# Two planes of queries stored at once, the sample item in one pass, a third output tile, and weight loads on another queue

## The chip, the cores and the metric

One core of a Trainium2 chip. The metric is the device time of one execution in microseconds (us); lower is better. The kernel before has a median of 3264.86 us in three runs (3264.8 to 3269.89).

## What is computed

A two-layer encoder step on 2048 prompt frames and 64 new frames ("sample") that follow 2048 past frames held in caches. Model width 1024, 16 heads of 64, all in float32. Layer A attends within bands of chunks (softmax with a bias by distance); layer B is a stick-breaking attention over shared keys and values.

```python
def band_attend(q, k, v, q_pos, k_pos, rel_bias):      # layer A
    s = jnp.einsum('bqhd,bkhd->bhqk', q, k).astype(jnp.float32) * SCALE
...
    s = s + rel_bias[:, rel].astype(jnp.float32)[None]
...
    p = jax.nn.softmax(s, axis=-1).astype(v.dtype)
    return jnp.einsum('bhqk,bkhd->bqhd', p, v)

def sb_block(q, k, v, q_pos, k_pos):                   # layer B
    z = jnp.einsum('bqhd,bkhd->bhqk', q, k).astype(jnp.float32) * SCALE
    mask = (k_pos[None, :] < q_pos[:, None])[None, None]
    log_fail = jnp.where(mask, jax.nn.log_sigmoid(-z), 0.0)
    later = jnp.flip(jnp.cumsum(jnp.flip(log_fail, -1), axis=-1), -1) - log_fail
    w = jnp.where(mask, jnp.exp(jax.nn.log_sigmoid(z) + later), 0.0)
    return jnp.einsum('bhqk,bkhd->bqhd', w.astype(v.dtype), v)
```

Each layer: an RMS norm, projections to q, k, v and a gate, attention, output times SiLU(gate), an output projection and the residual. The outputs are y for prompt and sample and the new key and value rows of both layers.

## The kernel before

Every float32 operand of a matmul is split in a rounded part (hi) and its rest (lo), so a product is two or three matmuls. Heads are taken in eight pairs (HP). The stages follow one another: A's projections (0 to 690 us of the span), A's attention (690 to 1310), B's projections (1310 to 2015), B's attention (2015 to 3156) and the last output tiles. Projections write q, k, v and gates to scratch in DRAM; attention loads them back.

**Scratch and stores.** q has three planes in DRAM: hi, lo, and hi once more (`lay`, `put` at L234), so that the two halves of a query tile can each be loaded as two neighbouring planes (`load_q`, L523: partitions 0 to 63 get hi and lo, 64 to 127 get lo and hi). `put` issues one DMA for a plane: three for q, two for k. The projections keep a half of the frames for one pair in tiles `sh` and `sl` (pool `st`, five buffers, L367); the cache's keys are turned on PE (`ps_c`) and split into `kh` and `kl` (`stage_cache`, L431).

**Attention.** Each attention runs in two passes, first the frame groups (1, 0) of 512, then (3, 2), over all head pairs. An `item` is a head, a group and (in B) a chunk of keys: scores `z` on PE, then softmax or a scan, turns of the weights (`wt`) on PE, splits `ph`/`pl` by ACT and DVE, products `acc` on PE. `gate_steps` (L603) closes a head: its `shift` moves half of `acc` into `otmp` and, in A, the other half into the output tile `ot` (two buffers), which after the gate is stored (`o_a<-ot`). The 64 new frames are the sample item, one for each head pair. In A it stands in the second pass, with its own bias rows `bs` (L1206) and queries `qs`. In B, `SAMPLE` (L40) divides it: in the first pass it meets the new frames' keys and the newest 512 of the cache (chunks 4 and 3), keeps the carry of its scan and a sum, and in the second pass it meets the other three chunks.

**Work beside it.** Projections that only the second pass needs are "late jobs" (`late_job`, L737): `load` fetches weights `lwh` and `lwl`, `some` multiplies into `ps_j`, `out` makes a gate `sg` or a split tile `sp` and stores it, and in A `add_back` and `token_rows` make the rows `lkn` of an output. In B the late weights were cut in the projections and lie in DRAM; they are loaded from ACT's queue. A class `Beat` deals steps out between items at a set rate.

**What sets the order.** A scheduler orders the instructions of each engine from program order and an estimate of times; within the attentions some are kept in program order. Loads and most stores go out from SP through `Queue` (load L135, store L128); L237 is `put`'s own DMA, and a helper records all the other operations as L91. Each DMA is counted on one of eight counters in turn, so an issue waits until the DMA eight before it on the same queues has landed; an instruction that must wait stops all that stand behind it on its engine. The names DMAHW0 to DMAHW7 below are these counters.

Of the kernel before, what the change touches and what calls it, by code (L numbers as in the profile page):

```python
# [16 lines left out]
P = 128  # L17
# [19 lines left out]

SEEN = 3

SAMPLE = {(1, 0): [4, 3], (3, 2): [2, 1, 0]}  # L40

DEFER = dict(a=[("k", hp) for hp in range(HP)], b=[(k, hp) for k in "gq" for hp in range(HP)])
KEPT = "b"
# [5 lines left out]
HOLD = dict(a=1, b=2)  # L49

STEP = 2
BEHIND = 2

SETTLE = 5
# [47 lines left out]
def encoder_step(ctx: ExitStack, tc: tile.TileContext, a: dict, o: dict):  # L102
# [70 lines left out]
    for L, rows in (("a", CACHE_A), ("b", PAST)):  # L173
        lay[L] = dict(


            q=[dram.tile([3, P, T], F32R, name=f"q_{L}{i}") for i in range(HP)],
            k=[dram.tile([2, P, T + rows], F32R, name=f"k_{L}{i}") for i in range(HP)],

            v=dram.tile([T + rows, H, P], F32R, name=f"v_{L}"),  # L180
            g=[dram.tile([P, T], F32, name=f"gate_{L}{i}") for i in range(HP)],

            o=[dram.tile([HP, P, CH if g < GROUPS else NS], F32, name=f"o_{L}{g}") for g in range(GROUPS + 1)],

            w={x: dram.tile([2, P, NK, P], F32R, name=f"w_{L}{x[0]}{x[1]}") for x in DEFER[L] if L in KEPT},
        )
# [44 lines left out]
            mm(out, sh(k), ml(k), start=False, stop=False)  # L231
            mm(out, sl(k), mh(k), start=False, stop=(k == NK - 1))

    def put(L, kind, hp, s, cols, part, by=nc.sync.dma_start):  # L234

        for i in (0, 2) if kind == "q" and s == 0 else (s,):
            by(f32(lay[L][kind][hp][i, :, cols]), f32(part))  # L237


    def projections(L, x_of, begin, w_v, cv, gv, out_v, jobs, first, prompt, sample, stages):  # L240
        with (
# [122 lines left out]
                                nc.scalar.dma_start(vraw[1 + r0 : 1 + r0 + n, cols], vn[:n])  # L364


            with tc.tile_pool(name=f"st_{L}", bufs=5) as spool, tc.tile_pool(name=f"t_{L}", bufs=2) as pool:  # L367
                for j, (kind, w, c0, g) in enumerate(jobs):
                    for hp in range(HP):
                        for _ in range(-(-len(stages) // (len(jobs) * HP - j * HP - hp))):  # L370
                            stages.pop(0)(pool)

                        home, tag = (pool, "wr") if hp % 2 else (opool, "og")
                        raw = home.tile([P, NK, P], F32, name="wraw", tag=tag, bufs=1)
                        c = c0 + hp * P
                        wh = opool.tile([P, NK, P], F32R, name="wh", tag="oh", bufs=2)
                        wl = opool.tile([P, NK, P], F32R, name="wl", tag="ol", bufs=2)

                        with tc.issue_after(first_copy.ins) if j == 0 and hp < 2 else nullcontext():
                            nc.scalar.dma_start(raw, w[:, c : c + P].rearrange("(k p) c -> p k c", p=P))  # L380
                            scaled_split(wh, wl, raw, g)
                        if (kind, hp) in lay[L]["w"]:
                            for i, part in enumerate((wh, wl)):
                                nc.sync.dma_start(f32(lay[L]["w"][kind, hp][i]), f32(part))
                        for hf, (r0, n, chunks) in enumerate(HALVES):
                            xh, xl = xs[hf]
                            if hf and (kind, hp) in DEFER[L]:

                                continue
                            if kind == "g":  # L390
                                sg = spool.tile([P, 1088], F32, name="sg", tag="st")
                            else:
                                sh = spool.tile([P, 1088], F32R, name="sh", tag="st")
                                sl = spool.tile([P, 1088], F32R, name="sl", tag="st")
                            for c, m in chunks:
                                ps = psum.tile([P, CH], F32, name="ps_t", tag="mm", bufs=5)
                                mm3(
                                    ps[:, :m],
                                    lambda k: wh[:, k],
                                    lambda k: wl[:, k],  # L400
                                    lambda k: xh[:, k, c : c + m],
                                    lambda k: xl[:, k, c : c + m],
                                )
                                if kind == "g":
                                    act.activation(sg[:, c : c + m], ps[:, :m], AF.Silu)
                                else:
                                    split(sh[:, c : c + m], sl[:, c : c + m], ps[:, :m])
                            if kind == "g":
                                nc.sync.dma_start(lay[L]["g"][hp][:, r0 : r0 + n], sg[:, :n])
                                continue  # L410
                            for s, part in enumerate((sh, sl)):
                                put(L, kind, hp, s, slice(r0, r0 + n), part[:, :n])
                            if kind == "k":

                                cols = slice(hp * P, hp * P + P)
                                for c in range(0, HALF, CH):
                                    b = hf * HALF + c - first
                                    if b >= 0:
                                        kf = pool.tile([P, CH], F32, name="kf", tag="kf", bufs=2)
                                        part = slice(c, c + CH)  # L420
                                        gps.tensor_tensor(kf, f32(sh[:, part]), f32(sl[:, part]), ALU.add)
                                        natural(pool, kf, 0, P, 4, prompt[b : b + CH, cols])
                                if hf == 0:
                                    kf = pool.tile([P, CH], F32, name="kf", tag="kf", bufs=2)
                                    part = slice(NEW, NEW + NS)
                                    gps.tensor_tensor(kf[:, :NS], f32(sh[:, part]), f32(sl[:, part]), ALU.add)
                                    natural(pool, kf, 0, NS, 1, sample[:, cols])
# [3 lines left out]
    def stage_cache(L, hp, c, pool):  # L431
# [4 lines left out]
        ps = bank("ps_c")  # L436
        for j in range(4):
            flip(ps[:, j * P : j * P + P], kr[:, j])
        kh = pool.tile([P, CH], F32R, name="kh", tag="kh", bufs=1)
        kl = pool.tile([P, CH], F32R, name="kl", tag="kl", bufs=1)  # L440
        split(kh, kl, ps)
        for s, part in enumerate((kh, kl)):
            put(L, "k", hp, s, to, part)
        if L == "b":
            return
        vr = pool.tile([P, 4, 2, DH], F32, name="vr", tag="vr", bufs=2)
# [76 lines left out]
    def load_q(L, pool, hp, h, q0):  # L523

        there(L, "q", hp, q0)
        q = pool.tile([P, 2, CH], F32R, name="q", tag="q", bufs=3)
        src = f32(lay[L]["q"][hp][:, h * DH : h * DH + DH, place(q0) : place(q0) + CH]).rearrange("s d t -> d s t")
        for s in range(2):
            queue.load(f32(q[s * DH : s * DH + DH]), src[:, s : s + 2])
        return q  # L530

    def load_gate(L, pool, hp, q0):
# [27 lines left out]
    class Sample:  # L560
# [9 lines left out]
        def queries(self, hp):  # L570
            q = self.q[hp % 3]
            for h in range(2):
                rows = slice(h * DH, h * DH + DH)
                src = f32(lay[self.L]["q"][hp][0:2, rows, NEW : NEW + NS])
                queue.load(f32(q[rows, :, rows]), src.rearrange("s d t -> d s t"))
            return q

# [25 lines left out]
    def gate_steps(L, pool, acc, h, c0, n, gt, sums, hp, g):  # L603
# [3 lines left out]

        def shift():
            if "ot" not in sums:
                sums["ot"] = pool.tile([P, CH], F32, name="ot", tag="ot", bufs=2)  # L610
            sums[h] = pool.tile([P, CH], F32, name="otmp", tag="otmp", bufs=1)
            act.activation(sums[h][mine, :n], acc()[other, c0 : c0 + n], AF.Copy)
            if L == "a" and n > NS:
                act.activation(sums["ot"][mine, :n], acc()[mine, c0 : c0 + n], AF.Copy)
# [122 lines left out]
    def late_job(L, kind, w, c0, g, hp, x2, first, prompt, rows_pool):  # L737
        st = {}

        def load():  # L740
# [5 lines left out]
            st["wl"] = opool.tile([P, NK, P], F32R, name="lwl", tag="ol", bufs=2)  # L746
            if L in KEPT:
                for i, part in enumerate((st["wh"], st["wl"])):
                    act.dma_start(f32(part), f32(lay[L]["w"][kind, hp][i]))

        def cut(k0):
            ks = slice(k0, k0 + STEP)
# [12 lines left out]
        def out(c):  # L765
# [7 lines left out]
            else:  # L773
                sp = opool.tile([P, 2, CH], F32R, name="sp", tag="xr", bufs=2)
                split(sp[:, 0], sp[:, 1], ps)
                for s in range(2):
                    put(L, kind, hp, s, at, sp[:, s], queue.store)
                st[c] = sp
            if c + CH == HALF:
                done_late.add((L, kind, hp))  # L780

        def add_back(c):

            st["kn"] = rows_pool.tile([P, CH], F32, name="lkn", tag="lkn", bufs=1)
            gps.tensor_tensor(st["kn"], f32(st[c][:, 0]), f32(st[c][:, 1]), ALU.add)

        def token_rows(c):
# [306 lines left out]
    with (  # L1094
# [106 lines left out]
        def sample_item(hp):  # L1201
            st, sums = {}, {}

            def one():

                bs = pool.tile([P, 576], F32, name="bs", tag="bs", bufs=1)  # L1206
                for h in range(2):
                    queue.load(bs[h * DH : h * DH + DH], biasd[hp][0:DH, h, 0:576])
                q = new.queries(hp)
# [61 lines left out]
    with (  # L1271
# [127 lines left out]
        def items():  # L1399
            for part in ORDER:  # L1400
                for hp in range(HP):
                    kv = {}
                    for g in part:
# [8 lines left out]
                                yield item(hp, g, h, q, gt, sums, kv[c], acc, carry, c)  # L1412
                        if hp == HP - 1:
                            beat.when_summed(partial(summed, g))
                    yield sample_item(hp, SAMPLE[part])
            beat.when_summed(partial(summed, GROUPS))

        def summed(g):
# [137 lines left out]
```

## Time and profile before

| | |
|---|---|
| Median of three runs | 3264.86 us |
| Profiled execution | 3263.8 us, span 3262.0 us |
| Granted TensorE clock, mean | 0.996 |
| DMA traffic | 688.41 MB |
| HBM read, written | 408.78 MB, 276.07 MB |

The span runs from the first to the last instruction that the profiler saw. PE is TensorE's matmuls and PEld its weight loads, DVE is VectorE, ACT ScalarE, POOL GpSimd, and SP the engine that issues most DMAs; SPq and ACTq are queue rows, where a duration is that of issuing and not of the transfer. A row of the timeline has its start, its duration, engine and line, operation, what it writes and reads, and in brackets the idle time of the engine ahead of it and what ended that. A landing time runs from a DMA's issue to its last byte.

### The profile page before, as it was taken

The numbers are of one execution on the slowest core, as the hardware profiler recorded it, in microseconds if no ns is written. First come the engines' busy times: TensorE is split into PE (matmuls) and PEld (weight loads), VectorE is DVE, ScalarE is ACT, GpSimd is POOL, SyncE is SP. The second block draws the span as 40 slices with busy tenths as digits, with TensorE's granted clock in tenths as the row PEclk, the third lists the DMA queues.
The fourth block names the chain that finished last, engine by engine and source line by source line (L and its number), as shares of the span: only waits on it lengthen the run. The fifth ranks groups of instructions, "written<-read, shape, count | busy, mean of one in ns | idle before, by whom it ended". The sixth has DMA issues, their size and how long they took to land.

```text
span 3262.0 us, 53645 instructions
## 1 busy us (share of the span) xinstructions
PE 3197.6 (98%) x17928; PEld 2783.9 (85%) x17928; DVE 1885.5 (58%) x3786; ACT 1709.4 (52%) x3719; POOL 1289.7 (40%) x1950
## 2 busy tenths in 40 slices
PE   8999999999998999999999999999999999999999
PEld 7889999988887898878899998888888888888877
DVE  4235431157778776232044332888878888888873
ACT  5234222258878776143143442666656666666662
POOL 3001110035655554020044200344467777777761
PEclk9999999999999999999999999999999999999999
DMA  6359993388899983453299999987735566355423
GB/s 204 121 185 368 351 333 122 118 251 219 235 266 258 254 231 121 167 185 130 106 349 352 350 353 336 254 219 215 214 117 164 167 203 193 116 144 143 137 72 120
DMA packets 464891, 688.41 MB, mean 211 GB/s; under 512 B 51445, under 2 KB 261397, under 8 KB 464614
## 3 DMA queue, kind: packets, MB, share of 16 engines
q1 hardware_dynamic: 398246, 608.68, 60.0%
q10 hardware_dynamic: 66368, 76.29, 7.3%
q8 instruction: 143, 2.34, 0.3%
q14 instruction: 134, 1.10, 0.1%
HBM read 408.78 MB, written 276.07 MB: 210 GB/s over the span
## 4 chain that ended last, share of the span: by engine, by line
PE 79%; issue 7%; DVE 7%; DMA 3%; ACT 2%; POOL 1%; SPq 0%; ACTq 0%; POOLq 0%; DVEq 0%
PE ps_t L91 24%; PE ps_v L91 11%; PE acc L91 11%; PE z L91 10%; PE wt L91 9%; PE ps_j L91 7%; PE ps_o L91 5%; DVE s L91 3%; DVE pl L91 2%; PE ps_tr L91 1%; DMA woraw<-in_w_out_a 1%; ACT ph L91 1%; PE ps_c L91 1%; POOL s L91 0%; PE ps_n L91 0%
## 5 line engine op out<-in xcount | busy, mean ns | idle before, releaser
L91 DVE TENSOR_TENSOR pl<-wt,ph 128x512 fp32r<-128x512 f32 (+1 forms) x864 | 550.6, 653 | 107.4 <-ACT ph L91 104.2
L91 ACT ACTIVATE ph<-wt 128x512 fp32r<-128x512 f32 (+1 forms) x864 | 484.4, 577 | 183.9 <-PE wt L91 170.6
L91 PE MATMUL ps_t<-x_own,wh 128*128 128x362 f32 (+1 forms) x2304 | 567.6, 327 | 0.0
L91 PE MATMUL wt<-ident,s 128*128 128x128 f32 x3472 | 549.5, 274 | 11.1 <-DVE pl L91 8.7
L91 PEld LDWEIGHTS wt<-ident,s 128*128 128x128 f32 x3472 | 416.4, 140 | 85.6 <-DVE pl L91 12.9
L91 ACT ACTIVATE f<-z 128x512 f32<-128x512 f32 (+4 forms) x680 | 355.8, 536 | 192.9 <-PE z L91 129.5
L91 PEld LDWEIGHTS ps_t<-x_own,wh 128*128 128x128 f32 x2304 | 405.1, 188 | 1.8
L91 POOL TENSOR_TENSOR s<-f,s 128x256 f32<-128x256 f32 x416 | 360.2, 867 | 103.2 <-DVE s L91 98.3
L91 PE MATMUL acc<-ph,vt 128*128 128x512 f32 (+3 forms) x1088 | 375.3, 379 | 10.6 <-ACT ot L91 9.0
L91 PE MATMUL ps_t<-x_own,wl 128*128 128x362 f32 (+1 forms) x1152 | 376.8, 327 | 0.0
L91 PE MATMUL z<-kt,q 128*128 128x512 f32 (+3 forms) x1280 | 373.3, 378 | 2.9 <-ACT f L91 2.6
L91 PE MATMUL acc<-pl,vt 128*128 128x512 f32 (+3 forms) x1088 | 362.7, 367 | 8.2 <-DVE pl L91 7.6
L91 POOL TENSOR_SCALAR s<-s,rc 128x640 f32<-128x640 f32 (+5 forms) x264 | 199.1, 758 | 388.4 <-DMA keys<-k_a 193.9
L91 PE MATMUL ps_o<-big,oh 128*128 128x512 f32 x1088 | 336.2, 392 | 0.0
L91 DVE TENSOR_TENSOR_SCAN s<-two,s,own 128x256 f32<-128x256 f32 x408 | 299.7, 737 | 35.5 <-POOL two L91 34.1
L91 POOL TENSOR_TENSOR two<-f 128x256 f32<-128x256 f32 x416 | 259.3, 625 | 150.8 <-ACT f L91 130.7
L91 PE MATMUL ps_j<-big,lwh 128*128 128x512 f32 x768 | 247.4, 398 | 7.6 <-DVE sg L91 7.0
L91 PEld LDWEIGHTS z<-kt,q 128*128 128x128 f32 x1280 | 219.9, 190 | 32.2 <-ACT f L91 10.0
L91 PE MATMUL ps_t<-big,wh 128*128 128x512 f32 x768 | 239.0, 391 | 0.0
L91 PEld LDWEIGHTS ps_o<-big,oh 128*128 128x128 f32 x1088 | 202.4, 188 | 41.1 <-DVE pl L91 0.2
L91 PEld LDWEIGHTS acc<-pl,vt 128*128 128x128 f32 x1088 | 193.6, 190 | 41.0 <-DVE pl L91 25.7
L91 DVE CUSTOM_DVE_ANT_0 s<-z,bias 128x640 f32<-128x640 f32 (+4 forms) x256 | 184.6, 732 | 72.5 <-PE wt L91 50.6
(148 smaller groups left out, 5527.5 us busy)
## 6 DMA issues: line engine op xcount, KB each, us to landing
vt<-v_b SPq DMA_DIRECT2D x80, 512.0 KB, 4.9
v_b<-vs SPq DMA_DIRECT2D x64, 512.0 KB, 5.7
q<-q_a SPq DMA_DIRECT2D x128, 256.0 KB, 6.0
q<-q_b SPq DMA_DIRECT2D x128, 256.0 KB, 4.4
vt<-v_a SPq DMA_DIRECT2D x48, 512.0 KB, 7.9
kt<-k_b SPq DMA_DIRECT2D x96, 256.0 KB, 6.6
keys<-k_a SPq DMA_DIRECT2D x80, 256.0 KB, 7.3
v_a<-vs ACTq DMA_DIRECT2D x32, 512.0 KB, 2.7
```

The lines of the kernel that those rows point to most:

```text
L91: ins = op(*args, **kwargs)
```

## The change

- q in scratch has two planes, hi and lo. Both halves of a query tile are loaded from the same two planes, so partitions 64 to 127 now hold hi and lo too. `put` stores hi and rest of a tile by one DMA; in the projections they are the halves of one tile `both` (two buffers), in `stage_cache` of one tile `ks`, in late jobs of `sp`, which it was before. A gate's two halves lie in one tile.
- B's sample item is wholly in the second pass, with chunks 4, 3, 2, 1, 0, and none of it in the first.
- A's output tile `ot` has three buffers, B's two as before.
- B's late weights `lwh` and `lwl` are loaded from SP's queue, not ACT's.
- `lkn`, the late key rows, and `bs`, the sample's bias rows in A, share one buffer.

```diff
-SAMPLE = {(1, 0): [4, 3], (3, 2): [2, 1, 0]}
+SAMPLE = {(3, 2): [4, 3, 2, 1, 0]}
...
+OT = dict(a=3, b=2)
...
-            q=[dram.tile([3, P, T], F32R, name=f"q_{L}{i}") for i in range(HP)],
+            q=[dram.tile([2, P, T], F32R, name=f"q_{L}{i}") for i in range(HP)],
...
-    def put(L, kind, hp, s, cols, part, by=nc.sync.dma_start):
-
-        for i in (0, 2) if kind == "q" and s == 0 else (s,):
-            by(f32(lay[L][kind][hp][i, :, cols]), f32(part))
+    def put(L, kind, hp, cols, parts, by=nc.sync.dma_start):
+
+        by(f32(lay[L][kind][hp][:, :, cols]).rearrange("s p t -> p s t"), f32(parts))
...
-            with tc.tile_pool(name=f"st_{L}", bufs=5) as spool, tc.tile_pool(name=f"t_{L}", bufs=2) as pool:
+            with tc.tile_pool(name=f"st_{L}", bufs=2) as spool, tc.tile_pool(name=f"t_{L}", bufs=2) as pool:
...
-                                sg = spool.tile([P, 1088], F32, name="sg", tag="st")
+                                if hf == 0:
+                                    gates = spool.tile([P, 2, 1088], F32, name="gates", tag="st")
+                                sg = gates[:, hf]
                             else:
-                                sh = spool.tile([P, 1088], F32R, name="sh", tag="st")
-                                sl = spool.tile([P, 1088], F32R, name="sl", tag="st")
+                                both = spool.tile([P, 2, 1088], F32R, name="both", tag="st")
+                                sh, sl = both[:, 0], both[:, 1]
...
-                            for s, part in enumerate((sh, sl)):
-                                put(L, kind, hp, s, slice(r0, r0 + n), part[:, :n])
+                            put(L, kind, hp, slice(r0, r0 + n), both[:, :, :n])
...
-        kh = pool.tile([P, CH], F32R, name="kh", tag="kh", bufs=1)
-        kl = pool.tile([P, CH], F32R, name="kl", tag="kl", bufs=1)
-        split(kh, kl, ps)
-        for s, part in enumerate((kh, kl)):
-            put(L, "k", hp, s, to, part)
+        ks = pool.tile([P, 2, CH], F32R, name="ks", tag="ks", bufs=1)
+        split(ks[:, 0], ks[:, 1], ps)
+        put(L, "k", hp, to, ks)
...
-        for s in range(2):
-            queue.load(f32(q[s * DH : s * DH + DH]), src[:, s : s + 2])
+        for x in range(2):
+            queue.load(f32(q[x * DH : x * DH + DH]), src)
...
-                sums["ot"] = pool.tile([P, CH], F32, name="ot", tag="ot", bufs=2)
+                sums["ot"] = pool.tile([P, CH], F32, name="ot", tag="ot", bufs=OT[L])
...
-                    act.dma_start(f32(part), f32(lay[L]["w"][kind, hp][i]))
+                    sp.dma_start(f32(part), f32(lay[L]["w"][kind, hp][i]))
...
-                for s in range(2):
-                    put(L, kind, hp, s, at, sp[:, s], queue.store)
+                put(L, kind, hp, at, sp, queue.store)
...
-            st["kn"] = rows_pool.tile([P, CH], F32, name="lkn", tag="lkn", bufs=1)
+            st["kn"] = rows_pool.tile([P, 576], F32, name="lkn", tag="bs", bufs=1)[:, :CH]
...
-                bs = pool.tile([P, 576], F32, name="bs", tag="bs", bufs=1)
+                bs = rpool.tile([P, 576], F32, name="bs", tag="bs", bufs=1)
...
-                    yield sample_item(hp, SAMPLE[part])
+                    if part in SAMPLE:
+                        yield sample_item(hp, SAMPLE[part])
```

PE's matmuls are the same in number. The places where order matters are these three.

ACT's order at the start of B's attention. `ks`/`kh` is the last cache tile, `both` the last projection tile, `sg` the first late gate, `ends` a copy for B's output, `f` the first scores' sigmoid; `w_bq` and `w_bg` are late weights of q and of the gate in DRAM. Before:

```order
L91 DMA lwh<-w_bq_149 128x1024 [waits DMAHW6_49,DMAHW1_49,DVE_49]
L91 DMA lwl<-w_bq_149 128x1024 [waits DMAHW2_49,DMAHW1_49]
L91 ACTIVATE kh<-ps_c 128x512 [waits DMAHW3_49,DVE_49,PE_49]
L91 ACT_TABLE_LOAD
L91 ACTIVATE sg<-ps_j 128x512 [waits PE_49]
L91 DMA lwh<-w_bg_142 128x1024 [waits DMAHW4_49,DMAHW1_49,PE_49]
L91 DMA lwl<-w_bg_142 128x1024 [waits DMAHW2_49,DMAHW0_49,PE_49]
L91 ACTIVATE sg<-ps_j 128x512 [waits PE_49]
L91 ACTIVATE ends<-ps_e 128x136 [waits DMAHW6_49,DMAHW5_49,DMAHW7_49,DMAHW4_49,DVE_49]
L91 ACTIVATE f<-z 128x128 [waits PE_49]
```

ACT's order there now:

```order
L92 ACTIVATE both<-ps_t 128x362 [waits PE_49]
L92 ACTIVATE ks<-ps_c 128x512 [waits DMAHW4_49,DVE_49,PE_49]
L92 ACTIVATE both<-ps_t 128x362 [waits PE_49]
L92 ACT_TABLE_LOAD
L92 ACTIVATE sg<-ps_j 128x512 [waits PE_49] x2
L92 ACTIVATE ends<-ps_e 128x136 [waits DMAHW3_49,DMAHW6_49,DMAHW2_49,DVE_49]
L92 ACTIVATE f<-z 128x128 [waits DVE_49,PE_49]
L92 ACTIVATE f<-z 128x256 [waits PE_49]
```

The four weight loads are gone from ACT's order, and the two `sg` follow one another.

SP's order at the same place; `q_b`, `k_b`, `v_b` and `gate_b` are scratch. Before:

```order
L237 DMA q_b_118<-sl 128x1088 [waits DMAHW2_49,DVE_49]
L135 DMA q<-q_b_111 64x2x512 [waits DMAHW3_49]
L135 DMA kt<-k_b_119 64x2x512 [waits DMAHW4_49]
L135 DMA kt<-k_b_119 64x2x512 [waits DMAHW5_49]
L135 DMA vt<-v_b 128x4x256 [waits DMAHW6_49]
...
L237 DMA k_b_126<-kh 128x512 [waits DMAHW6_49,Activation_49]
L237 DMA k_b_126<-kl 128x512 [waits DMAHW7_49,DVE_49]
L128 DMA gate_b_128<-sg 128x512 [waits DMAHW0_49,DVE_49]
L128 DMA gate_b_128<-sg 128x512 [waits DMAHW3_49,DVE_49]
```

SP's order there now:

```order
L92 DMA lwh<-w_bq_149 128x1024 [waits DMAHW0_49,PE_49]
L136 DMA q<-q_b_111 64x2x512 [waits DMAHW1_49,PE_49]
L237 DMA k_b_126<-ks 128x2x512 [waits DMAHW2_49,DVE_49]
L237 DMA q_b_118<-both 128x2x1088 [waits DMAHW3_49,DVE_49]
L136 DMA q<-q_b_111 64x2x512 [waits DMAHW4_49]
L136 DMA kt<-k_b_119 64x2x512 [waits DMAHW5_49]
L136 DMA kt<-k_b_119 64x2x512 [waits DMAHW6_49]
L136 DMA vt<-v_b 128x4x256 [waits DMAHW7_49]
L92 DMA lwl<-w_bq_149 128x1024 [waits DMAHW0_49]
...
L92 DMA lwh<-w_bg_142 128x1024 [waits DMAHW3_49,PE_49]
L92 DMA lwl<-w_bg_142 128x1024 [waits DMAHW4_49,PE_49]
```

The stores of the last cache tile and the last query tile stand ahead of the first key loads, `lwl` of the queries behind the first values, and the next gate's weights behind the rest. Of before seven rows of key, value and query loads are left out, of now ten, which are the same kinds a gate's store and load, and the last norm's weights.

SP's order in A's second pass, around the store of `lkn`; `bias_168` is the bias of the second head pair, `gate_a_100` the new frames' gate of the third. Before, the piece of SP's order with the `bs` loads:

```order
L135 DMA keys<-k_a_91 64x2x512 [waits DMAHW1_49]
L135 DMA keys<-k_a_91 64x2x512 [waits DMAHW2_49]
L135 DMA bs<-bias_168 64x576 [waits DMAHW3_49,DVE_49]
L135 DMA bs<-bias_168 64x576 [waits DMAHW4_49]
L135 DMA vt<-v_a 128x4x256 [waits DMAHW5_49,PE_49]
L91 DMA woraw<-in_w_out_a 128x1024 [waits DMAHW6_49]
```

And the piece with the `lkn` store, some twenty rows later:

```order
L128 DMA o_a_108<-ot 128x512 [waits DMAHW3_49,Pool_49]
L128 DMA out_a_k_p<-lkn 128x4x128 [waits DMAHW4_49,Activation_49]
L135 DMA gt<-gate_a_99 128x512 [waits DMAHW5_49]
...
L135 DMA q<-q_a_83 64x2x512 [waits DMAHW2_49,PE_49]
L128 DMA o_a_110<-ot 128x64 [waits DMAHW3_49,Pool_49]
L135 DMA q<-q_a_83 64x2x512 [waits DMAHW4_49]
L135 DMA gs<-gate_a_100 128x64 [waits DMAHW5_49]
L135 DMA q<-q_a_83 64x2x512 [waits DMAHW6_49,PE_49]
```

SP's order there now:

```order
L129 DMA o_a_108<-ot 128x512 [waits DMAHW1_49,Pool_49]
L129 DMA out_a_k_p<-lkn 128x4x128 [waits DMAHW2_49,Activation_49]
L136 DMA gt<-gate_a_99 128x512 [waits DMAHW3_49]
...
L136 DMA q<-q_a_83 64x2x512 [waits DMAHW0_49,PE_49]
L129 DMA o_a_110<-ot 128x64 [waits DMAHW1_49,Pool_49]
L136 DMA q<-q_a_83 64x2x512 [waits DMAHW2_49]
L136 DMA gs<-gate_a_100 128x64 [waits DMAHW3_49]
L136 DMA bs<-bias_168 64x576 [waits DMAHW4_49]
L136 DMA bs<-bias_168 64x576 [waits DMAHW5_49]
```

The `bs` loads of the second pair stand behind the store of `lkn`, whose buffer they now share; before they stood some 25 rows ahead of it.

More of the change, by code (lines that the diff above doesn't have):

```diff
@@ L573, in queries @@
                 rows = slice(h * DH, h * DH + DH)
-                src = f32(lay[self.L]["q"][hp][0:2, rows, NEW : NEW + NS])
+                src = f32(lay[self.L]["q"][hp][:, rows, NEW : NEW + NS])
                 queue.load(f32(q[rows, :, rows]), src.rearrange("s d t -> d s t"))
```

## The prediction

> **What bounds the kernel now.** I read the busy times first, then the span in windows by stage, then what TensorE (PE) waited for, and then the timeline around its two longest waits.
>
> ```profile
> span 3262.0 us, 53645 instructions
> PE 3197.6 (98%) x17928; PEld 2783.9 (85%) x17928; DVE 1885.5 (58%) x3786; ACT 1709.4 (52%) x3719; POOL 1289.7 (40%) x1950
> ```
>
> PE is busy for 98% of the span. The change takes no matmul away and adds none, so what it can save is idle PE time and time at a low granted clock; work saved on another engine counts only where PE waits for that engine. The windows (start and end, length, busy time and instructions of PE, PEld, DVE, ACT and POOL, then granted clock, DMA share, GB/s) show where idle time is.
>
> ```profile
> 1000.00:1050.00 50.00, 41.02 (x254) 36.98 (x255) 36.17 (x89) 36.20 (x79) 24.01 (x26) 0.90 0.99 269
> 1900.00:1950.00 50.00, 50.00 (x315) 49.90 (x314) 19.45 (x49) 20.29 (x54) 0.00 (x0) 1.00 0.99 351
> 2000.00:2050.00 50.00, 42.64 (x213) 37.11 (x212) 9.16 (x19) 8.17 (x16) 1.00 (x3) 0.90 0.94 286
> 2300.00:2350.00 50.00, 49.24 (x297) 42.04 (x296) 43.08 (x73) 33.59 (x71) 24.84 (x43) 1.00 0.67 190
> 2800.00:2850.00 50.00, 49.37 (x272) 40.64 (x271) 43.09 (x68) 32.35 (x64) 39.91 (x73) 1.00 0.33 96
> ```
>
> In B's projections (1900) PE is full although the DMA engines are at 0.99; in both passes of B's attention (2300, 2800) it misses 0.6 to 0.8 us in 50. Only the windows at 1000 and 2000 lose 7 to 9 us, and both show a clock of 0.90. PE's waits there (total, times, longest) have one large row each, the first in A's second pass and the second at B's start:
>
> ```profile
> PE acc L91 <- ACT ot L91: 8.4, 3, 6.5
> PE ps_j L91 <- DVE sg L91: 7.0, 1, 7.0
> ```
>
> So the sum has two places, and a list of edits that should cost nothing.
>
> **B's start: the late weights leave ScalarE's queue.**
>
> ```profile
> 2021.21 0.60 ACT L91 ACTIVATE sg<-ps_j 128x512 f32<-128x512 f32 x1 [3.53 <-PE ps_j L91]
> 2038.57 0.33 ACTq L91 DMA_DIRECT2D lwl<-w_bg  x1
> 2038.94 0.60 ACT L91 ACTIVATE sg<-ps_j 128x512 f32<-128x512 f32 x1 [17.13 <-DMA q<-q_b]
> 2040.32 1.22 PE L91 MATMUL ps_j<-big,lwh 128*128 128x512 f32 x2 [6.98 <-DVE sg L91]
> 2035.00:2040.00 5.00, 0.00 (x0) 0.00 (x0) 0.43 (x1) 0.60 (x1) 0.00 (x0) 0.60 1.05 225
> 2040.00:2045.00 5.00, 4.68 (x11) 3.72 (x12) 1.40 (x6) 0.73 (x3) 0.82 (x2) 0.50 1.01 392
> 2045.00:2050.00 5.00, 5.00 (x22) 4.07 (x22) 2.61 (x6) 1.35 (x3) 0.19 (x1) 0.88 0.93 325
> ```
>
> Two weight loads stand between two gates (sg) in ScalarE's (ACT's) order, and the second could be issued only at 2038.57, after a load on SP (q) had landed. The second sg stood behind them for 17.13 us, its PSUM bank stayed taken, and PE idled 6.98 us. After it the clock is 0.50 until 2045 and for 1.2 us more (0.88 over 5 us is (1 - 0.88) x 5 / 0.5): 4.68 + 1.2 = 5.9 us at half rate, which lose 2.9. The Trainium skill ("TensorE: Matmul & The Clock Gate", Part 1: The HAM clock gate) says that about 3.4 us of sustained work restore full rate; by that the loss would be about 1.7 us and the sum 1.2 us smaller. The trace disagrees on the length, and I go by it.
>
> In the changed order the two sg follow one another with nothing between, and the loads stand on SP, so the wait goes, with the clock loss behind it. PE also waited for a cache tile, whose last turn now stands between projection matmuls:
>
> ```profile
> 2015.09 0.63 PE L91 MATMUL ps_c<-ident,kr 128*128 128x128 f32 x4 [0.38 <-DMA kr<-in_cache_b_k]
> 2017.82 3.01 SPq L135 DMA_DIRECT2D kt<-k_b  x2
> DMA to landing us min/median/max: 9.1/9.9/10.7
> 2026.54 0.60 PE L91 MATMUL ps_e<-ident,vcur 17*128 17x17 f32 x7
> 2027.94 0.62 PE L91 MATMUL ps_j<-big,lwh 128*128 128x512 f32 x2
> 2043.74 0.52 POOL L91 MEMSET own_s<- 128x512 f32 x1 [182.72 <-DMA gate_b<-sg]
> ```
>
> What is late next? PE's first scores (z) now stand four matmuls behind ps_e; the fourth began at 2027.94 in before, so PE comes to them at about 2028.1. They need two key halves. SP's rows ahead of the keys are about as many as before, and the DMAs that the keys wait for are now early stores, so I put the issue of the second half at 2018.4. With the landing times above (the keys' own row of that stretch) it is there at 2027.5 to 2029.1: a wait of 0 to 1.0. The late query weights' second half (lwl) stands three rows on, at about 2019.6; PE needs it at about 2030, it lands at 2028.7 to 2030.3: 0 to 0.3 more. The first turn of weights needs own_s, whose clearing stood behind the last stores of projection tiles; these now stand ahead of the loads (issued near 2016.5, down by about 2027 at the same rate), so own_s is made some 15 us sooner: 0 to 1.3. I take 1.3 in all, half of the 2.6. **Term: 7.0 + 2.9 + 0.4 - 1.3 = 9.0 us less**, between 7.7 and 10.3.
>
> **A's second pass: a third buffer for ot, and a shared buffer for the late rows.**
>
> ```profile
> 1005.94 1.12 SPq L128 DMA_DIRECT2D o_a<-ot  x1
> 1008.13 0.60 ACT L91 ACTIVATE ph<-wt 128x512 fp32r<-128x512 f32 x1
> 1015.37 0.59 ACT L91 ACTIVATE ot<-acc 64x512 f32<-64x512 f32 x1 [6.65 <-DMA o_a<-ot]
> 1015.00:1020.00 5.00, 3.98 (x12) 3.55 (x13) 1.29 (x4) 4.63 (x10) 2.94 (x4) 0.50 0.68 182
> 1020.00:1025.00 5.00, 5.00 (x32) 4.74 (x31) 4.49 (x11) 3.53 (x9) 1.19 (x1) 0.78 0.80 176
> ```
>
> ACT waited 6.65 us for the store of an ot whose buffer it wanted, and PE behind it. With three buffers the one wanted has long been stored. The three waits of PE are 8.4 us, and the half clock behind the long one is 3.98 us plus (1 - 0.78) x 5 / 0.5 = 2.2, so 3.1 lost: 11.5 to gain. But the bias rows of the sample item (bs) now share one buffer with the late rows (lkn), and the scheduler put their loads behind that store:
>
> ```profile
> 1007.15 0.39 SPq L128 DMA_DIRECT2D out_a_k_p<-lkn  x1
> DMA to landing us min/median/max: 8.8/8.8/8.8
> 1016.63 0.56 SPq L135 DMA_DIRECT2D gs<-gate_a  x1
> 976.63 1.19 SPq L135 DMA_DIRECT2D bs<-bias  x2
> DMA to landing us min/median/max: 4.8/7.0/9.2
> 1022.87 0.76 DVE L91 CUSTOM_DVE_ANT_0 s<-z,bs 128x576 f32<-128x576 f32 x1 [0.51 <-PE z L91]
> ```
>
> The lkn store goes out at 1007.15 and is down 8.8 us later, at 1016.0. In the order of after, gs and then both bs loads follow within ten rows of it, behind a query load that waits for this store. In the trace of before that gs went out at 1016.63, so bs can go out at 1017.2, not at 976.63 as before, and lands 4.8 to 9.2 us later: 1022.0 to 1026.4, at the median 1024.2. VectorE (DVE) used bs at 1022.87, and without the stall would come to it 7.4 us sooner, at 1015.5. It then waits 6.5 to 10.9 us, in order, with the splits behind it on which PE's products wait. So one stall takes the place of the other: 11.5 - 8.7 leaves 2.8, and -0.3 if PE's clock falls by half again. **Term: 1.5 us less**, about the middle; between 5.0 less (early landing) and 3 more (late landing with the half clock).
>
> For the first pair the same sharing is just in time:
>
> ```profile
> 956.91 0.40 SPq L128 DMA_DIRECT2D out_a_k_p<-lkn  x1
> 975.28 0.75 DVE L91 CUSTOM_DVE_ANT_0 s<-z,bs 128x576 f32<-128x576 f32 x1
> ```
>
> Store 956.91 + 8.8 + bs 9.2 is 974.9, against 975.28. Cost 0 here; what slower landings make of it is the third rival. The other loads held back behind bs there (output weights, queries) move by some 3 us and are used later.
>
> **Edits that I cost at nothing.** Two planes instead of three, and one store for both: 160 store instructions and 8 x (544 + 512) + 8 x 544 + 16 x 256 KB = 17 MB less. PE is full through the projections (row 1900), so a lighter DMA has nothing to shorten; the bounds are 0 and the 0.4 us above. The pool of double tiles holds four halves instead of five: a tile must be stored before the one after next is written, and five PSUM banks stand between. Bound: nothing to one landing, 9 us, once; the trace shows no wait for such a slot and I take 0.
>
> The sample item of B moves to the second pass whole. Its scans, products and splits run beside a full PE:
>
> ```profile
> L91 DVE TENSOR_TENSOR total<-total,acc 128x128 f32<-128x128 f32 x32 | 9.0, 280 | 13.5 <-ACT total L91 8.9 <-PE acc L91 4.5
> L91 DVE COPY carry<-s x8: 126/134/145, 2083.9 to 2364.2; 128x1 f32<-128x1 f32 x8
> L91 DVE TENSOR_TENSOR_SCAN s<-two,s,own 128x256 f32<-128x256 f32 x408 | 299.7, 737 | 35.5 <-POOL two L91 34.1
> L91 DVE TENSOR_TENSOR pp<-wt,pp 128x256 fp32r<-128x256 f32 x80 | 31.4, 409 | 2.7 <-ACT pp L91 2.3
> ```
>
> It drops 16 of the 32 adds and the 8 carry copies: 16 x 0.28 + 8 x 0.134 = 5.6 us of DVE. Each of eight pairs brings one more wide scan (0.74) and three or so splits (0.41), near 2.2 us, to a DVE that is at 43.1 of 50. PE's matmuls of the item move along, so both engines get more in the pass, and DVE stays below PE. If that cover were gone, 8 x 2.2 = 17.8 us would show.
>
> **Sum.** The profiled execution took 3263.8 (span 3262.0 and 1.8 around it), 1.06 below the median of 3264.86. 3263.8 - 9.0 - 1.5 = 3253.3; against the median 3254.4. I say 3254, with its own range of 3249 to 3260 from the two terms' ends.
>
> **The rivals.**
> - *Both stalls go* (0.16): bs comes in time because the lkn store leaves earlier. Then 10.3 + 11.5 go: 3243. For it: the third buffer's wait is gone in any case. Against it: the landing times add up to 1022 at the least.
> - *Only the queue changes* (0.16): the loads are late on SP as they were on ACT, and PE idles at its scores or at the late weights instead. Then 3264.9 - 1.5 = 3263. For it: DMA share 1.01 to 1.05 from 2035. Against it: sg itself is freed whatever the loads do. By the Trainium skill ("DMA: Bandwidth & Descriptors", Issuing engines are not separate DMA queues) the loads run on the same 16 DMA engines whoever issues them; the rows agree that landing is no faster, but what stalled here was ACT's own order.
> - *Slower by the shared buffer* (0.06): with the slowest landing of that stretch for store and load,
>
> ```profile
> DMA to landing us min/median/max: 8.9/9.5/12.9
> ```
>
> (output weights, 970 to 1030) bs is down at 956.91 + 25.8 = 982.7 in the first pair, 7.4 late, and at 1007.15 + 12.9 + 0.6 + 12.9 = 1033.6 in the second, 10.7 after its use of before, the old stall included. So A is 18.1 longer and B's start 9.0 shorter: 3264.9 + 9.1 = 3274. It decides once store and load together exceed 18.4 us in the first pair.
> - *Slower by the second pass* (0.06): DVE sets its pace, +17.8 - 10.5: 3272. Against it: 43.1 of 50.
>
> **How the numbers follow.** The forecast has 0.56. About 0.2% (6.5 us) is what a measurement of this kernel tells from no change: faster is below 3258.3, slower above 3271.4. Nine tenths of the forecast and the first rival are faster, 0.66; the rest of it and the second are the same, 0.22; the last two are slower, 0.12. The range goes from the first rival, 3242, to 3266, beyond the second, and leaves out the two slow cases.
>
> **What would show it.** ACT's wait of 17.13 us and PE's of 6.98 at ps_j gone, and no clock of 0.50 near 2040; ACT's wait for the ot store gone, and in its place DVE waiting for bias loads near 1016 to 1024; PE as full as before in 1900 and in the second pass. It is wrong if PE waits over 3 us for keys or late weights at B's start, if DVE is late in B's second pass, or if bs is no wait at all.

## The result and the profile after

The changed kernel takes 3275.81 us at the median of seven runs, the kernel before 3266.91 us in the same comparison: a ratio of 1.0032, with an interval of 1.0022 to 1.0042. It is slower by 9 us where 10.5 less had been forecast, and lies outside the range. A profile shows one execution: the seven of the changed kernel lie between 3272.70 and 3279.95, and the profiled one took 3272.70; e1's profile below is of its longest, 3269.49 at a median of 3265.70. So what two profiles differ by in a stage, a few us, can be the execution's and not the edit's, and the medians decide.

The page of the changed kernel, its span and busy times:

```profile
span 3270.8 us, 53223 instructions
...
PE 3200.2 (98%) x17928; PEld 2783.6 (85%) x17928; DVE 1869.6 (57%) x3762; ACT 1708.8 (52%) x3719; POOL 1291.3 (39%) x1950
```

The span grew by 8.8 us. DVE does 15.9 us less work, and the span is longer all the same; PE executes as many matmuls and is 6.2 us longer idle and 2.6 longer busy. The windows by stage show where. The columns are as in the prediction: start and end, length, then PE's busy time first. The stages are A's attention, B's start, most of B's first pass, B's second pass, and the tail. Before:

```profile
690.00:1310.00 620.00, 597.33 (x3786) 533.49 (x3785) 458.61 (x1236) 480.79 (x1100) 335.46 (x384) 0.99 0.84 231
...
2026.00:2110.00 84.00, 75.52 (x409) 62.18 (x408) 56.67 (x96) 41.69 (x91) 32.01 (x58) 0.94 0.95 255
2110.00:2360.00 250.00, 247.21 (x1483) 211.97 (x1483) 212.41 (x353) 163.00 (x349) 112.70 (x193) 1.00 0.78 216
2360.00:3150.00 790.00, 777.31 (x4428) 643.15 (x4427) 664.82 (x1067) 528.77 (x1053) 589.48 (x1090) 1.00 0.50 148
3150.00:3254.00 104.00, 103.62 (x486) 85.96 (x485) 45.89 (x82) 33.96 (x76) 22.47 (x30) 1.00 0.38 121
```

The same windows of the changed kernel:

```profile
690.00:1310.00 620.00, 598.64 (x3791) 534.26 (x3790) 460.23 (x1239) 481.61 (x1100) 338.88 (x385) 0.99 0.85 232
...
2026.00:2110.00 84.00, 73.04 (x394) 60.01 (x392) 55.06 (x84) 41.33 (x86) 29.64 (x52) 0.96 0.87 234
2110.00:2360.00 250.00, 243.19 (x1417) 205.84 (x1416) 211.35 (x330) 160.74 (x332) 115.80 (x192) 1.00 0.68 187
2360.00:3150.00 790.00, 780.14 (x4479) 646.74 (x4478) 658.12 (x1063) 525.79 (x1065) 584.01 (x1089) 1.00 0.53 152
3150.00:3254.00 104.00, 99.71 (x475) 82.59 (x475) 47.03 (x84) 36.08 (x80) 24.89 (x35) 1.00 0.38 123
```

Length less PE's busy time is its idle time. It changes by -1.3, +2.5, +4.0, -2.8 and +3.9 us, 6.3 in all, so the stages left out add nothing: in these two executions A gains a little, B's start loses, the first pass and the tail lose, the second pass gains.

PE's waits from 2026 to 2110 in the changed kernel (engine and output, what it waited for; total, times, longest):

```profile
PE z L92 <- DMA q<-q_b: 7.2, 2, 5.8
PE z L92 <- ACT f L92: 1.4, 1, 1.4
PE acc L92 <- DVE pl L92: 1.0, 2, 0.5
PE wt L92 <- DVE s L92: 0.7, 1, 0.7
PE ps_j L92 <- DMA lwl<-w_bq: 0.4, 1, 0.4
```

The old row, ps_j waiting 7.0 us for the gate, is gone, and scores wait 7.2 us for queries. The chain of waits through that stretch (start, length, what held) says why they came late:

```profile
2022.42 9.04 DMA lwl<-w_bq
...
2036.47 9.11 DMA lwl<-w_bg
...
2051.05 6.55 DMA vt<-v_b
2057.61 11.60 DMA q<-q_b
2069.23 9.78 DMA q<-q_b
```

It is a chain of transfers, each of which holds for 6.6 to 11.6 us. In ten-us windows the DMA engines are full around the wait (from 2040 to 2050 their share was 0.68):

```profile
2050.00:2060.00 10.00, 9.45 (x51) 7.39 (x50) 8.01 (x13) 5.74 (x12) 6.13 (x11) 1.00 1.04 270
2060.00:2070.00 10.00, 4.16 (x21) 3.24 (x20) 3.96 (x6) 2.66 (x5) 0.00 (x0) 0.83 1.06 257
2070.00:2080.00 10.00, 8.62 (x50) 7.78 (x50) 6.84 (x11) 5.52 (x12) 0.00 (x0) 0.83 1.07 287
```

In B's first pass (2110 to 2360) PE's waits were these before, and behind them are the changed kernel's:

```profile
PE wt L91 <- DVE pl L91: 1.5, 4, 0.5
PE acc L91 <- DVE pp L91: 1.0, 4, 0.3
PE acc L91 <- DVE pl L91: 0.2, 1, 0.2
```

```profile
PE acc L92 <- DVE pl L92: 5.9, 11, 1.3
PE wt L92 <- POOL s L92: 0.4, 1, 0.4
```

Products of the prompt items wait for DVE's splits eleven times where they waited once. At two of the longest of these waits (PE returns at 2147.14 and 2333.66) the split stands in DVE's order behind a run of scans, 3.2 and 2.4 us long. And in the tail (from 3140) of the changed kernel:

```profile
PE ps_o L92 <- ACT oh L92: 2.5, 1, 2.5
PE wt L92 <- DVE pp L92: 1.0, 1, 1.0
PE wt L92 <- POOL rstd L92: 0.8, 1, 0.8
PE acc L92 <- DVE pl L92: 0.3, 1, 0.3
```

These rows but the last are new. ACT's rows around the longest of them:

```profile
3187.34 0.28 ACT L92 ACTIVATE total<-acc 128x128 f32<-128x128 f32 x1 [4.64 <-PE acc L92]
...
3190.06 1.15 ACT L92 ACTIVATE oh<-og 128x512 fp32r<-128x512 f32 x2
```

The split `oh` of the last big output tiles stands in ACT's order behind the sample item's sum, and that waits for the item's last products.

### The profile page after: what moved, and what is told of

The parts are those of the page before. It is cut to its first block, busy times and chain, and to the rows that moved or that the text cites. A ratio compares the mean times of both kernels' runs of the same rounds, so it can differ in the third digit from the quotient of the medians.

```text
span 3270.8 us, 53223 instructions
## 1 busy us (share of the span) xinstructions
PE 3200.2 (98%) x17928; PEld 2783.6 (85%) x17928; DVE 1869.6 (57%) x3762; ACT 1708.8 (52%) x3719; POOL 1291.3 (39%) x1950
## 3 DMA queue, kind: packets, MB, share of 16 engines
q14 instruction: 131, 1.07, 0.1%
## 4 chain that ended last, share of the span: by engine, by line
PE 76%; issue 8%; DVE 7%; DMA 5%; ACT 3%; POOL 1%; SPq 1%; ACTq 0%; POOLq 0%; DVEq 0%
PE ps_t L92 23%; PE ps_v L92 11%; PE acc L92 10%; PE z L92 9%; PE wt L92 8%; PE ps_j L92 6%; PE ps_o L92 5%; DVE s L92 3%; DVE pl L92 2%; PE ps_tr L92 1%; ACT ph L92 1%; DMA q<-q_b 1%; ACT s L92 1%; DMA keys<-k_a 1%; SPq L136 1%
## 5 line engine op out<-in xcount | busy, mean ns | idle before, releaser
L92 ACT ACTIVATE f<-z 128x512 f32<-128x512 f32 (+3 forms) x680 | 356.6, 536 | 207.5 <-PE z L92 147.9
```

The source lines that it names most:

```text
L92: ins = op(*args, **kwargs)
```

## The experiments

Two questions: does the moved sample item cost the time (theory S), or do the late weights in SP's queue (theory W)? And what holds B's start? "Before" is the kernel before in the same comparison: 3266.91 us beside the changed kernel, 3265.2 to 3265.7 beside the others.

| Kernel | Median us | Ratio to before, interval |
|---|---|---|
| changed kernel | 3275.81 | 1.0032, 1.0022 to 1.0042 |
| e1: changed, sample item divided again | 3265.70 | 0.9997, 0.9988 to 1.0006 |
| e2: changed, late weights on ACT again | 3278.11 | 1.0039, 1.0026 to 1.0052 |
| e3: before, sample item moved | 3280.66 | 1.0050, 1.0037 to 1.0062 |
| e4: before, late weights on SP | 3264.40 | 0.9996, 0.9987 to 1.0004 |
| e5: changed, last pair's sample item first | 3269.97 | 1.0015, 1.0006 to 1.0024 |
| e6: e1 without loads of the weights' rest | 3260.19 | 0.9988, 0.9979 to 0.9998 |
| e7: e1, four query and four key tiles | 3264.23 | 0.9997, 0.9988 to 1.0006 |
| e8: before, two planes and merged stores | 3263.96 | 0.9997, 0.9988 to 1.0006 |
| e9: before, A's two edits | 3265.16 | 0.9998, 0.9989 to 1.0007 |
| e10: e1, norm late, four query tiles | 3264.14 | 0.9996, 0.9987 to 1.0004 |
| e11: e10, late rows in their own buffer | 3274.63 | 1.0026, 1.0017 to 1.0035 |

**e1, the sample item divided again.**

```diff
-SAMPLE = {(3, 2): [4, 3, 2, 1, 0]}
+SAMPLE = {(1, 0): [4, 3], (3, 2): [2, 1, 0]}
```

> The changed kernel with B's sample item divided between the passes as before (chunks 4 and 3 in the first, 2 to 0 in the second). Theory S (the moved sample item is the cost: its early loads hold up the first query loads of B, and a longer last item stretches the tail): PE's waits of 7.2 us for queries near 2069 and 2079 go, and so do the 4.3 us of idle PE after 3150; about 3256 us, some 20 below the changed kernel and 10 below before. Theory W (the late weights in SP's queue are what holds the queries up): the tail's 4.7 us come back, the waits for queries stay at 7; about 3271 us.

It takes 10 us off and ends at the time of before, neither at 3256 nor at 3271. PE's waits of 2026 to 2110:

```profile
PE z L92 <- DMA q<-q_b: 9.2, 2, 8.2
```

The wait for queries is not the moved item's: it stays, at 9.2 us. What came back is the tail (PE's waits there fall from 4.6 to 1.6 us in all) and the first pass, where from 2110 to 2360 PE waits 1.4 us. So both theories were right on the tail, W on the queries, and neither had priced the first pass.

**e3, the sample item moved alone.** The edit is that of the change, `SAMPLE` and the `if` around the first pass's item.

> The kernel before with B's sample item moved to the second pass, nothing else. Theory S: 4.7 us more in the tail, and some us more in waits for queries or keys at B's start beside the old stall at the gate; 3272 to 3278 us. Theory W: the tail alone, 4.7 us more; about 3271.6 us, with no new wait at B's start. If the item's scans made the second pass slower, idle PE between 2370 and 3150 would rise above the 11.9 us of before.

Alone it costs 15 us, more than S expected, though no wait for queries appears. The old wait for the gate grows to 9.8 us:

```profile
PE ps_j L91 <- DVE sg L91: 9.8, 1, 9.8
PE acc L91 <- DVE pl L91: 1.0, 3, 0.5
```

In the first pass (2110 to 2360) products wait for splits again, and the tail has the changed kernel's rows (and 1.1 us of waits for ACT's sigmoid). The first pass:

```profile
PE acc L91 <- DVE pl L91: 7.3, 13, 1.2
```

The second pass isn't slower for it: its idle time falls from 12.7 to 10.1 us.

**e2 and e4, the late weights' queue.**

```diff
-                    act.dma_start(f32(part), f32(lay[L]["w"][kind, hp][i]))
+                    sp.dma_start(f32(part), f32(lay[L]["w"][kind, hp][i]))
```

e4 makes this edit on the kernel before, e2 takes it back in the changed one.

> The kernel before with B's late weights loaded from SP's queue, nothing else. Theory S: the stall of 7.0 us at the gate and the half clock behind it go, and no wait for queries takes their place; about 3258 us (9 less). Theory W: PE waits 5 to 7 us for queries or keys between 2050 and 2080 instead; about 3267 us.

> The changed kernel with B's late weights loaded from ACT's queue as before. Theory S: the second gate stands behind weight loads again (a wait of some 15 us on ACT, 5 to 7 us of idle PE near 2040), the waits for queries near 2069 stay in part and the tail stays; 3274 to 3283 us. Theory W: PE's waits for queries go, the idle time near 2040 returns; about the changed kernel's 3276 us, with 7 us idle at 2040 and under 2 us at 2060 to 2080.

e4's wait for the gate goes, and the time stays. Its waits of 2026 to 2110:

```profile
PE z L91 <- DMA q<-q_b: 4.2, 1, 4.2
PE wt L91 <- issue: 1.7, 1, 1.7
PE ps_j L91 <- DMA lwl<-w_bq: 1.1, 1, 1.1
PE ps_j L91 <- DMA lwh<-w_bq: 0.9, 1, 0.9
```

Queries and late weights hold PE for 6.2 us in place of 7.0. That is theory W's account; its time, 3267, was 2.6 us too high, and S's 3258 was 6.4 too low. In e2 both stand side by side, 6.4 us idle near 2038 and 3.4 for queries near 2078, and the time is that of the changed kernel. To take the edit alone in or out moves nothing that these runs can tell. The Trainium skill ("DMA: Bandwidth & Descriptors", Issuing engines are not separate DMA queues) says that DMAs run on the same 16 DMA engines whichever engine starts them. The traces agree: from 2010 to 2090 the late weights landed in 4.8 to 9.9 us from ACT's queue (e2) and in 4.3 to 11.9 us from SP's (the changed kernel), so the other queue brings them no sooner.

**e6 and e7, what holds B's start.** Is it bytes (theory D) or too few query tiles (theory Q)? Both start from e1.

```diff
-                for i, part in enumerate((st["wh"], st["wl"])):
+                for i, part in enumerate((st["wh"],)):
```

In e6 `wl` is `wh` in B.

> The first experiment's kernel (sample item divided as before, late weights on SP) without the loads of the late weights' rest in B: products use the rounded part in its place, so gates and queries of the late half are less exact, and 16 loads of 512 KB are left out, about 1.5 MB of them before 2085. Theory D (bytes: the DMA engines are full from 2020 to 2080, and what must be loaded sets when B gets going): PE's waits for queries near 2068 and 2084, 9 us in its profile, fall under 3 us; 6 to 9 us less than the first experiment, about 3257 to 3260 us. Theory Q (buffers: a query tile is asked for only when one of three is free, too late whatever else is loaded): waits of 6 us or more stay; 3263 to 3266 us.

```diff
-        q = pool.tile([P, 2, CH], F32R, name="q", tag="q", bufs=3)
+        q = pool.tile([P, 2, CH], F32R, name="q", tag="q", bufs=4 if L == "b" else 3)
...
-        KV, SB = 5, 12
+        KV, SB = 4, 12
```

> The first experiment's kernel with four query tiles in B instead of three, and four key and value tiles instead of five, which makes the room. Theory Q: queries are asked for one item sooner, and PE's waits for them fall under 3 us; about 3257 us. Theory D: the wait at B's start moves to another load (keys or queries) and stays at 7 us or more in all; 3264 to 3268 us. Fewer key tiles may add waits for keys later in the first pass.

PE's waits of 2026 to 2110 in e6, and then in e7:

```profile
PE z L92 <- ACT f L92: 2.9, 2, 2.8
```

```profile
PE z L92 <- ACT f L92: 4.1, 1, 4.1
```

Either edit removes the wait for queries: fewer bytes bring a query sooner, a fourth tile asks for it sooner. e6 is 5.5 us faster than e1 by the medians, somewhat less than D's 6 to 9. In e7 another wait comes up, scores for ACT's sigmoid, 4.1 us, and with four value tiles waits for values of up to 2.1 us come in the second pass; by the medians that is 1.5 us less than e1, within the intervals. So the theories aren't rivals here: PE waits since a query is asked for late and the full DMA engines then take some 10 us to bring it (9.8 and 11.6 in the chain above). Why the median of e7 gains so little, when PE's idle time from 2026 to 2110 is 6.1 us and e1's 12.6, is not settled; e1's profile, of its longest execution, may show more of that wait than most.

**e5, the tail.** In the changed kernel the last head pair's sample item is put ahead of that pair's prompt items.

```diff
+                    early = hp == HP - 1 and part in SAMPLE
+                    if early:
+                        yield sample_item(hp, SAMPLE[part])
                     for g in part:
...
-                    if part in SAMPLE:
+                    if part in SAMPLE and not early:
```

> The changed kernel with B's sample item of the last head pair placed ahead of that pair's prompt items in the second pass. Theory T (the tail is longer because five chunks of a sample item are the last work): idle PE after 3150 falls from 4.3 to under 1 us, the wait of 2.5 us for ACT's oh goes; about 4 to 5 us less than the changed kernel, 3271 us. Rival: the last prompt item then ends the pass, its output tile is stored and loaded later, and PE waits for it there: 3275 us or more.

As theory T expected: 5.8 us less by the medians (the intervals meet at 1.0022 to 1.0024), 0.7 us idle from 3150 to 3254, and still 4 us above the kernel before. The wait for `oh` is gone from the tail (PE's two longest sums there):

```profile
PE z L92 <- ACT f L92: 1.1, 2, 0.8
PE acc L92 <- DVE pl L92: 0.9, 3, 0.4
```

**e8, planes and merged stores alone.** The change without the edits to `SAMPLE`, `OT`, the late weights' queue and the shared buffer.

> The kernel before with two planes of queries and merged stores, nothing else. Theory N (stores were hidden): within 2 us of before, 3264 to 3268 us, projections as full as before, the stall at the gate near 2040 still there. Rival: two double tiles are too few for the projections' stores, and PE idles there by several us; or the lighter queue lets B start sooner, 3 to 9 us less.

As expected: 17 MB and 160 stores less change nothing that can be told. The stall near 2040 is still there, 6.2 us.

**e9 and e11, A's two edits.**

> The kernel before with A's two edits alone: three output tiles, and one buffer shared by the late rows and the bias rows. Theory R (one wait takes the other's place): ACT's 6.65 us for the store of an output tile go, VectorE waits 4 to 7 us for bias rows near 1017 to 1025 instead; 3264 to 3267 us. Rival: the third tile's gain stays in part, 3 us or more less than before; or the shared buffer costs more than it saves, over 3268.

No change, as expected: one wait has taken the other's place. DVE's step of the second head pair in the changed kernel, in e9, and PE behind it in the changed kernel:

```profile
1021.47 0.76 DVE L92 CUSTOM_DVE_ANT_0 s<-z,bs 128x576 f32<-128x576 f32 x1 [4.48 <-DMA bs<-bias]
1022.29 1.17 PE L92 MATMUL z<-keys,q 128*128 128x320 f32 x3 [4.04 <-DVE mn L92]
```

```profile
1020.54 0.76 DVE L91 CUSTOM_DVE_ANT_0 s<-z,bs 128x576 f32<-128x576 f32 x1 [5.15 <-DMA bs<-bias]
```

ACT's `ot` no longer waits for a store, and DVE waits for the bias rows. How long differs between executions of the same edits: 4.5 us in the changed kernel, 5.2 to 9.6 in e1, e2, e6, e7, e9 and e10, 11.2 in e5. PE's idle time in A's attention is 20.2 to 26.2 us in these profiles, and 22.7 to 23.8 in those without the edits (before, e3, e4, e8). e11 gives the late rows their own buffer, with one softmax tile less for room, on top of e10 (which has e1's order, `gf` issued behind the first pass's loads, four query tiles and ten scan tiles).

> The first experiment's kernel with the last norm's weights (512 KB) loaded only behind the first pass's last loads, and four query tiles in B in place of three (ten scan tiles in place of twelve make the room; keys and values keep five). Theory D with Q (full engines make the query loads slow, and three tiles make them late): PE's waits for queries near 2068 and 2084 go and no wait for values comes in the second pass, as it did with four value tiles; 5 to 9 us less than the first experiment, 3257 to 3261 us. Rival: ten scan tiles hold VectorE up in both passes; 3265 us or more.

> The kernel of the run just described with A's late rows in a buffer of their own again, beside three output tiles (eight softmax tiles in place of nine make the room). Theory R: with the shared buffer gone, VectorE's wait for bias rows goes, and the store wait doesn't return: PE's longest idle time in A falls from 4 to 6 us to under 2 and the low clock near 1020 goes; 7 to 11 us less than that run, 3247 to 3253 us. Rival: eight softmax tiles or another wait takes the place again; within 3 us of that run.

e10 loses its wait for queries too, but its second pass waits more (PE's idle time there rises from 12.8 us in e1 to 15.5), and by the medians it is at 3264.1, not below 3261. In e11 the long wait in A is gone, as expected, and the time is 10 us worse than e10's, which neither the theory nor the rival expected. PE's waits of 690 to 1310 there:

```profile
PE wt L92 <- DVE pl L92: 7.7, 11, 2.0
PE z L92 <- DVE mn L92: 6.0, 11, 1.0
PE acc L92 <- ACT ph L92: 4.9, 6, 1.2
PE acc L92 <- ACT ot L92: 3.3, 9, 1.0
```

In place of one long wait there are many small ones through A. That they come of the softmax tile less is likely but not shown, as no run takes that tile away alone. So the third output tile's worth without the shared buffer, beside nine softmax tiles, remains unmeasured. No version that computes everything is told apart from the kernel before as faster; e6, which leaves the rest of the late weights out, is.

## Why the prediction was wrong

Two steps of the sum failed: the look at what is late next at B's start stopped too early, and the moved sample item was put at nothing. No rival has both. The rival of the shared buffer gives 3274, close to the measured time, but by 18 us in A that did not come; its number is luck.

- **B's start, -9.0, measured +2.5 of idle time** (8.5 to 11.0 from 2026 to 2110), and e4, the queue's edit alone, no change that can be told. The removal was as described: the two gates follow one another and no weight load stands between. The step that failed is "What is late next?". I priced the first scores, the weights' rest and own_s, within 2.6 us, and there it held: PE waits 0.4 us for `lwl`, 0.7 for the first scan, nothing for keys. I stopped at the first item. The queries of the items behind it are asked for only when one of three tiles is free, come over the same full DMA engines, and without the stall PE reaches them before they land: it waits 7.2 us for them in the changed kernel, 4.2 in e4. The old stall had been their cover. The rival "only the queue changes" described this, at 0.16, and e4 shows it by itself. What spoke against it (that the gate is freed whatever the loads do) was true and beside the point.
- **The sample item at nothing, measured 10 us (e1) to 15 us (e3) by the medians.** The failed step is "runs beside a full PE": it looked at the pass that the item enters, and there it is right; the second pass idles less (9.9 us where it was 12.7), which refutes the rival of a second pass paced by DVE. (The price of that rival is also off: one scan and three splits are 0.74 + 3 x 0.41 = 1.97 us, not near 2.2, and eight times 2.2 is 17.6; nothing else hangs on it.) What the item left, and where it ends, were not priced. In the first pass the item's matmuls had stood beside prompt items whose products need DVE's splits; without them PE waits 5.9 us at products where it waited 0.2, and is idle 4.0 us more in all. At the end, the last pair's longer item delays ACT's split for the last output tiles: 3.9 us more idle, which e5 removes. And some 2.5 us are busy time: the 352 products of the sample items, 272 of them B's, take 54.5 us in all where they took 52.0, and A's 80 take 10.8 in both (here by groups of PE's instructions, before and after). The executions with the item moved (e2, e3, e5) have 54.7 to 54.9, e1 has 52.0.

```profile
L91 PE MATMUL acc<-pp,vt 128*128 128x128 f32 x352 | 52.0, 275 | 1.0 <-DVE pp L91 1.0
```

```profile
L92 PE MATMUL acc<-pp,vt 128*128 128x128 f32 x352 | 54.5, 279 | 0.4 <-ACT ot L92 0.4
```

- **A's second pass, -1.5, measured -1.3 of idle time.** That the two numbers agree is luck of the profiled execution: with the same edits e5 idles 4.8 us more there. The mechanism was right. One stall took the place of the other as worked out: bias rows were there at 1021.5, just ahead of the 1022.0 to 1026.4 of the forecast, and DVE, which came to them at 1017.0 and not at 1015.5, waited 4.5 us instead of 6.5 to 10.9 (other executions lie in that range: 7.0 in e1, 9.6 in e6). By e9's medians the net is nothing that can be told. The rival with the slowest landings did not come about.
- **Planes and merged stores at nothing: right**, by e8.

That the first pass's waits for DVE's splits come with the item's move is shown by putting it back (e1) and by moving it alone (e3). That the item's matmuls had given DVE the time to finish its scans is how I read it, and is not shown by itself. Not settled either: why e3 costs 5 us more on the kernel before than e1 gives back on the changed one. Its profile has a longer wait for the gate, 9.8 against 7.0 us. It also has a low clock in the tail, 0.83 from 3180 to 3190, that is 3.4 us at half rate and 1.7 lost; e2 has it too (0.90 and 0.92 from 3170 to 3190), while the changed kernel's profile has 1.00 behind the same waits. Each can be a part of it, and how often the changed kernel has that low clock is not known.

## What to carry to other kernels

A stall at the start of a stage is worth its length only if the data for the next items is there when it is gone; where the DMA engines are full, follow the loads of the second and third items, not only the first, before a stall is booked as a gain. When work is moved to a place where it is hidden, price three places: where it goes, what it was covering where it was, and whether it is now the last thing to finish. And a buffer shared to make room for another can hand the wait over to its new partner; the order of stores and loads on one queue shows it ahead of any run. Where executions of one kernel differ by 7 us, a gain of 1.5 us read from one profile of each kernel proves nothing by itself.

## What the runs showed of the hardware

The low clock behind a stall is shorter in some places than in others, and can stay away. After the wait that ended at 2069.35 in the changed kernel, the window from 2070 has 0.83, that is 3.4 us at half rate ((1 - 0.83) x 10 / 0.5), so about 4.1 us from PE's return; before, it was 5.9 us at 2040 and 6.2 at 1016. Behind the tail's waits of 1.0 and 0.8 us it was 3.4 us in e3 and nothing in the changed kernel. The 3.4 us of the Trainium skill ("TensorE: Matmul & The Clock Gate", Part 1: The HAM clock gate) is nearer to the shorter ones than to 5.9 and 6.2; which a stall will have was not to be told from these runs.

A load took longer where the DMA engines were full: a query load of 256 KB that was issued at 2015 in the changed kernel landed in 4.6 us, and one at 2058 took 11.6 us (the chain above); the DMA share was 0.61 from 2010 to 2020 and 1.04 to 1.07 from 2050 to 2080.
